# A third exponential tile and 15 KB more arena in a two-layer encoder kernel

## The chip, the cores and the metric

One NeuronCore of a Trainium2 chip runs the whole program. The metric is the device time of one execution in microseconds. Three executions of the kernel before took 1659.9, 1661.06 and 1663.4 us; the median, 1661.06 us, is the time before.

## What is computed

Two inputs A and B, each 1024 tokens by 1024 channels, pass through the same two layers. The reference, cut:

```
def even_layer(x, ...):
    h = rms_norm(x, norm_g)
    pu, pz, q, k, v, az = split(h @ w_in)           # 512, 512, 512, 128, 128, 512
    a_out = pool_mixer(pu, pool_w, pool_scale) * silu(pz)
    b_out = axial_gqa(q, k, v, q_g, k_g, tables) * silu(az)
    return x + concatenate([a_out, b_out]) @ w_out

def odd_layer(x, ...):
    h = rms_norm(x, norm_g)
    u, vv, z = split(h @ w_in, 3)
    vv = rms_norm(gelu(vv), sgu_g)
    sv = per chunk of 128 tokens, 8 groups: w_s @ vv + b_s
    return x + (gelu(u) * sv * silu(z)) @ w_out
```

The attention has 8 query heads of 64 channels on 2 key heads, full over the 1024 tokens, with normalised and rotated queries and keys. The pool mixer subtracts a token from the mean of a window (2, 4, 8 or 16 tokens) and mixes each group of 128 channels.

## The kernel before

**Numbers in two halves.** Each float32 operand of a matmul is scaled by a power of two and split into a float16 value and a float16 rest. A product takes three passes (`PASSES`, L383): high by high, high by rest, rest by high. The splitting is done by ScalarE (the rounding copy) and VectorE (the subtraction): L169 and L170 for weights, L365 and L366 for normalised inputs, L697 and L698 for probabilities, L753 to L756 for mixed values.

**Memory.** One large SBUF tile, the arena (`ARENA`, L33), holds nearly everything. `Arena.get` and `Arena.free` only note sizes and lifetimes; the kernel is traced, a planner (`make_plan`, `tried`, L76 to L116) gives each of the noted tiles an offset, and the kernel is traced again with them. The planner places large and long-lived tiles first, and each at the offset where the distance in time to the other users of that place is largest, counted up to 3.5% of the whole (`SLACK`); among equals it takes the lowest offset. The framework lays a wait wherever two tiles that share a place follow one another.

**Rings.** `consts_even` takes three rings out of the arena (L444 to L446), which live until the end of the second attention: transposed probabilities (3 tiles of 8 KB per partition), exponentials (`pf`, 2 tiles of 4 KB), and split probabilities (4 tiles of 4 KB). `Ring.get` hands the tiles out in turn.

**Attention.** `attention` (L660) runs four times for A and four times for B, each time for two heads, in rounds of 128 queries and one head: 16 rounds a call, 128 in all. A round is: four matmuls into a PSUM score tile of 128 by 1024 (L678; there are two such tiles), the maximum on VectorE (L684), the bias on ScalarE (L685), the exponential on ScalarE into a tile of the `pf` ring (L686), and a round later the split: a scaled row sum (L693), its reciprocal on VectorE (L695), the high half on ScalarE (L697), the rest on VectorE (L698), and a transposing transfer issued by SyncE (L699). For each 256 queries of the two heads 48 matmuls multiply values and probabilities (L710), and VectorE takes the result out (L714).

**Order.** Between the rounds `fill` (L335) runs chunks of other work out of a list by a nominal cost: projections, the pool mixer, norms of the other input, the output product of A, the beginning of its odd layer. Weights are fetched one block ahead (`Weights.fill`, L135): SyncE loads them (L153), VectorE takes the largest value (L252), and the two halves are made (L169, L170). All of the kernel's matmuls outside attention go through `mm` (L399). The order on each engine is not the order of the program text: the framework's scheduler lays it out ahead by its own estimate of times (`schedule_with_timeline_sim`, L1060), and each engine, and SyncE's queue of transfers, then keeps to it.

**After attention**, from about 920 us, come the rest of the odd layer's first product for A, the output product of B, and the odd layers of both.

SBUF also holds, at its low end, the space that the framework reserves for descriptors of transfers issued by GpSimd. The kernel before says nothing of it, and gets 16 KB per partition.

Of the kernel before, what the change touches and what calls it, by code (L numbers as in the profile page):

```python
# [10 lines left out]
F32 = mybir.dt.float32  # L11
# [9 lines left out]
P = 128  # L21
L = 1024
# [7 lines left out]
PAD = 8  # L30
W_PAD = L + 2 * PAD
RING = 96
ARENA = 186 * 1024  # L33
GRAIN = 512


class Arena:
# [3 lines left out]
    def __init__(self, nc, pool, plan=None):  # L41
        self.tile = pool.tile([P, ARENA // 4], F32, name="arena")
        self.nc, self.plan = nc, plan
        self.spans, self.held, self.now = [], {}, 0.0
# [45 lines left out]
def tried(spans, order, end):  # L90
    placed, plan = [], [None] * len(spans)
    for i in order:
# [3 lines left out]
        holes, last = [], 0  # L96
        for lo, hi in clash + [(ARENA, ARENA)]:
            if lo - last >= g:
# [101 lines left out]
class Kernel:  # L200
# [207 lines left out]
    def consts_even(self):  # L408
        nc = self.nc
        self.rope = {}  # L410
        cs = self.get([P, 2, NT, HD], F32)
        nc.sync.dma_start(out=cs, in_=self.rope_cs)
        ds = []
        for name, row in (("k", self.k_norm), ("q", self.q_norm)):
            g = self.tiny([P, 2, HD], keep="gain_" + name)
            nc.sync.dma_start(out=g[:, 0, :], in_=row.rearrange("(o n) -> o n", o=1).broadcast_to([P, HD]))
            gv = g[:, 0, :].rearrange("p (h s i) -> p h s i", h=2, s=2)
            gw = g[:, 1, :].rearrange("p (h s i) -> p h s i", h=2, s=2)
            for s in range(2):
                nc.vector.tensor_copy(out=gw[:, :, s, :], in_=gv[:, :, 1 - s, :])  # L420
            am = self.tiny([P, 1])
            self.amax(am, g[:, 0, :])
            d, s = self.scales(am, 1, 11, "g" + name, across=False)
            nc.vector.tensor_scalar(out=g, in0=g, scalar1=s[:, 0:1], scalar2=None, op0=ALU.mult)
            t = self.get([P, 2, NT, HD], F32, long=True)
            for i in range(2):
                nc.gpsimd.tensor_tensor(out=t[:, i], in0=cs[:, i], in1=g[:, i:i + 1, :].broadcast_to([P, NT, HD]), op=ALU.mult)
            self.rope[name] = t
            ds.append(d)
        self.free(cs)  # L430
        self.s_scale = self.tiny([P, 1], keep="s_scale")
        nc.vector.tensor_scalar(out=self.s_scale, in0=ds[0], scalar1=ds[1][:, 0:1], scalar2=HD ** -0.5, op0=ALU.mult, op1=ALU.mult)
        self.s_neg = self.tiny([P, 1], keep="s_neg")
        nc.vector.tensor_scalar(out=self.s_neg, in0=self.s_scale, scalar1=-1.0, scalar2=None, op0=ALU.mult)
        raw = self.get([P, 4, P], F32)
        nc.sync.dma_start(out=raw, in_=self.pool_w.rearrange("g c d -> c g d"))
        nc.vector.tensor_copy(out=self.pw[:, 0], in_=raw)
        nc.vector.tensor_tensor(out=self.pw[:, 1], in0=raw, in1=self.pw[:, 0], op=ALU.subtract)
        self.free(raw)
        self.pscale = self.tiny([P, 4], keep="pscale")  # L440
        nc.sync.dma_start(out=self.pscale, in_=self.pool_scale.rearrange("(g p) -> p g", p=P))
        self.edge = self.tiny([P, 4, 2, 8], keep="edge")
        nc.sync.dma_start(out=self.edge, in_=self.edges)
        self.pt = Ring(self, 3, [P, 2, NT, 256], F16)  # L444
        self.pf = Ring(self, 2, [P, L], F32)
        self.phl = Ring(self, 4, [P, 2, L], F16)  # L446

    def rotated(self, *args):
# [562 lines left out]
@with_exitstack  # L1011
def trunk_kernel(ctx: ExitStack, tc: tile.TileContext, args, order, plan):
    k = Kernel(ctx, tc, args, order, plan)
    k.run()
    k.arena.finish()
    return k.wts.order, k.arena.spans
# [32 lines left out]
def _trace(shapes, order=None, plan=None):  # L1049


    import concourse.bacc as _bacc

    nc = _bacc.Bacc("TRN2", target_bir_lowering=False, num_devices=1)
    args = {n: nc.dram_tensor("in_" + n, s, F32, kind="ExternalInput").ap() for n, s in shapes.items()}
    args["xs"] = [args.pop("x_prompt"), args.pop("x_sample")]
    args["outs"] = [nc.dram_tensor(f"out_{i}", (L, D), F32, kind="ExternalOutput").ap() for i in range(2)]
    noted = None
    try:
        with tile.TileContext(nc, schedule_with_timeline_sim=True) as tc:  # L1060
            noted = trunk_kernel(tc, args, order, plan)
            if plan is None:
                raise _Noted
    except _Noted:
        pass
    return nc, noted


def _planned(shapes):
    order, _ = _trace(shapes)[1]  # L1070
    return order, make_plan(_trace(shapes, order)[1][1])
# [15 lines left out]
```

## Time and profile before

| | before |
|---|---|
| median of three runs | 1661.06 us |
| the profiled execution, its span | 1660.36 us, 1658.3 us |
| PE busy | 1510.0 us, 91%, 11751 matmuls |
| PE weight load busy | 1025.5 us, 62% |
| DVE busy | 1064.1 us, 64% |
| ACT busy | 726.7 us, 44% |
| POOL busy | 121.1 us, 7% |
| data queue (SyncE) | 215.90 MB, 56.4% of 16 engines' span |
| mean granted TensorE clock | 0.963 |

PE is TensorE, DVE VectorE, ACT ScalarE, POOL GpSimd, SP SyncE. The profile is of one execution; its waits are worked out from semaphore events, and a wait for several things is put down to the one that came last. A mean over the span hides that the stages have different limits.

### The profile page before, as it was taken

The numbers are of one execution on the slowest core, as the hardware profiler recorded it, in microseconds if no ns is written. First come the engines' busy times: TensorE is split into PE (matmuls) and PEld (weight loads), VectorE is DVE, ScalarE is ACT, GpSimd is POOL, SyncE is SP. The second block draws the span as 40 slices with busy tenths as digits, with TensorE's granted clock in tenths as the row PEclk, the third lists the DMA queues.
The fourth block names the chain that finished last, engine by engine and source line by source line (L and its number), as shares of the span: only waits on it lengthen the run. The fifth ranks groups of instructions, "written<-read, shape, count | busy, mean of one in ns | idle before, by whom it ended". The sixth has DMA issues, their size and how long they took to land.

```text
span 1658.3 us, 28057 instructions
## 1 busy us (share of the span) xinstructions
PE 1510.0 (91%) x11751; PEld 1025.5 (62%) x11751; DVE 1064.1 (64%) x1613; ACT 726.7 (44%) x1121; POOL 121.1 (7%) x187
## 2 busy tenths in 40 slices
PE   2989899967779899999789899999979999998999
PEld 2745554646545777565468788554468655467888
DVE  7798999886897665798965754556660634344221
ACT  4366676766554555566655720224442513111000
POOL 2410010111100000010200200001100100000000
PEclk9999999978979999999899999999999999999999
DMA  9557787999866877787796453126511113224121
GB/s 237 122 120 151 148 149 148 197 202 181 182 134 146 191 182 170 158 162 145 191 213 155 127 186 99 42 77 140 127 52 39 39 38 102 70 90 140 64 84 52
DMA packets 497151, 217.69 MB, mean 131 GB/s; under 512 B 366336, under 2 KB 488704, under 8 KB 497024
## 3 DMA queue, kind: packets, MB, share of 16 engines
q1 hardware_dynamic: 497024, 215.90, 56.4%
q8 instruction: 92, 1.51, 0.4%
q14 instruction: 35, 0.29, 0.1%
HBM read 101.04 MB, written 24.12 MB: 75 GB/s over the span
## 4 chain that ended last, share of the span: by engine, by line
PE 37%; DVE 6%; DMA 5%; ACT 3%; issue 1%; POOL 0%; SPq 0%; DVEq 0%; ACTq 0%
PE bank L399 24%; PE ps_s L399 13%; DMA arena<-in_w_in_o 3%; DMA arena<-arena 1%; DVE arena L170 1%; ACT arena L169 1%; DVE arena L366 1%; DVE arena L364 1%; DMA arena<-in_w_out_e 1%; ACT arena L362 0%; DVE ring_weights L252 0%; DVE kept L252 0%; PE bank L710 0%; DVE arena L903 0%; DVE ring_attention L684 0%
## 5 line engine op out<-in xcount | busy, mean ns | idle before, releaser
L399 PEld LDWEIGHTS <-arena 128*128 128x128 f16 x9600 | 870.9, 99 | 458.7 <-DMA arena<-arena 34.6
L399 PE MATMUL bank<-arena 128*128 128x256 f16 (+2 forms) x8064 | 949.2, 279 | 47.7 <-DMA arena<-arena 14.0
L399 PE MATMUL ps_s<-arena 128*128 128x512 f16 x1536 | 335.5, 379 | 0.0
L169 ACT ACTIVATE arena<-arena,kept 128x1024 f16<-128x1024 f32 x108 | 122.2, 1144 | 327.1 <-DVE kept L281 125.7
L170 DVE SCALAR_TENSOR_TENSOR arena<-arena,kept 128x1024 f16<-128x1024 f32 x108 | 138.2, 1287 | 133.5 <-ACT arena L169 132.9
L698 DVE SCALAR_TENSOR_TENSOR arena<-arena,ring_attention 128x1024 f16<-128x1024 f32 x128 | 163.5, 1278 | 30.6 <-ACT arena L697 26.8
L686 ACT ACTIVATE arena<-ps_s,ring_attention,kept 128x1024 f32<-128x1024 f32 x128 | 153.8, 1201 | 38.9 <-DVE ring_attention L695 17.8
L678 PE MATMUL ps_s<-arena 128*128 128x512 f16 x512 | 138.7, 398 | 32.6 <-ACT arena L686 28.6
L684 DVE TENSOR_REDUCE ring_attention<-ps_s 128x1 f32<-128x1024 f32 x128 | 154.9, 1215 | 16.4 <-PE ps_s L678 15.8
L697 ACT ACTIVATE arena<-arena,ring_attention 128x1024 f16<-128x1024 f32 x128 | 145.8, 1141 | 36.8 <-DVE ring_attention L695 33.6
L784 DVE SCALAR_TENSOR_TENSOR arena<-bank,ring_dout,arena 128x512 f32<-128x512 f32 x64 | 47.6, 747 | 140.5 <-PE bank L399 139.6
L710 PE MATMUL bank<-arena 128*64 128x256 f16 x1536 | 110.1, 296 | 30.2 <-DMA arena<-arena 26.4
L710 PEld LDWEIGHTS <-arena 128*64 128x64 f16 x1536 | 93.5, 120 | 55.3 <-DMA arena<-arena 26.5
L252 DVE TENSOR_REDUCE ring_weights<-arena 128x1 f32<-128x1024 f32 x58 | 70.6, 1216 | 80.3 <-DMA arena<-in_w_in_o 36.4
L678 PEld LDWEIGHTS <-arena 128*128 128x128 f16 x512 | 48.1, 100 | 94.1 <-issue 47.2
L685 ACT ACTIVATE ring_attention<-ring_attention,kept 128x1 f32<-128x1 f32 x128 | 36.9, 290 | 132.8 <-DVE ring_attention L684 132.5
L364 DVE SCALAR_TENSOR_TENSOR arena<-arena,ring_norm 128x1024 f32<-128x1024 f32 x32 | 41.0, 1280 | 19.5 <-POOL ring_norm L318 19.3
L838 ACT ACTIVATE arena<-bank,ring_dvv 128x256 f32<-128x256 f32 x64 | 26.7, 467 | 56.3 <-PE bank L399 52.2
L362 ACT ACTIVATE arena<-arena 128x1024 f32<-128x1024 f32 x32 | 33.6, 1052 | 36.0 <-DMA arena<-in_x_prompt 13.9
L884 DVE SCALAR_TENSOR_TENSOR arena<-bank,kept,arena 128x512 f32<-128x512 f32 x32 | 22.9, 748 | 39.6 <-PE bank L399 39.6
L365 ACT CAST arena<-arena 128x1024 f16<-128x1024 f32 x32 | 33.3, 1040 | 33.9 <-DVE arena L364 33.7
L315 POOL TENSOR_SCALAR ring_norm<-ring_norm 128x1 f32<-128x1 f32 x32 | 12.7, 398 | 467.7 <-ACT arena L362 458.1
(104 smaller groups left out, 888.3 us busy)
## 6 DMA issues: line engine op xcount, KB each, us to landing
arena<-in_w_in_o SPq DMA_DIRECT2D x48, 512.0 KB, 4.1
arena<-in_w_in_e SPq DMA_DIRECT2D x36, 512.0 KB, 4.7
arena<-in_w_out_e SPq DMA_DIRECT2D x16, 512.0 KB, 5.2
x<-arena SPq DMA_DIRECT2D x32, 256.0 KB, 3.2
arena<-x SPq DMA_DIRECT2D x16, 512.0 KB, 4.3
arena<-x SPq DMA_DIRECT2D x32, 256.0 KB, 2.9
out<-arena SPq DMA_DIRECT2D x32, 256.0 KB, 2.1
mixed<-arena SPq DMA_DIRECT2D x14, 512.0 KB, 3.7
```

The costliest lines, as they stand in the source:

```text
L169: nc.scalar.activation(out=hi, in_=raw, func=AF.Copy, scale=s[:, 0:1])
L170: nc.vector.scalar_tensor_tensor(out=lo, in0=raw, scalar=s[:, 0:1], in1=hi, op0=ALU.mult, op1=ALU.subtract)
L252: self.nc.vector.tensor_reduce(out=out, in_=in_, axis=axis, op=ALU.max, apply_absolute_value=True)
L364: nc.vector.scalar_tensor_tensor(out=x, in0=x, scalar=r[:, 0:1], in1=gain[0], op0=ALU.mult, op1=ALU.mult)
L399: self.nc.tensor.matmul(out=o, lhsT=l, rhs=r, start=first and i == 0, stop=last and i == n - 1)
L678: nc.tensor.matmul(out=ps[:, half * 512:half * 512 + 512], lhsT=st.qT[j][:, tt, h, :], rhs=st.kT[:, 4 * half:4 * half + 4, kv, a, :], star ...
L684: nc.vector.tensor_reduce(out=m, in_=ps, axis=AX.X, op=ALU.max)
L686: nc.scalar.activation(out=p, in_=ps, func=AF.Exp, scale=self.s_scale[:, 0:1], bias=nb[:, 0:1], accum_out=ss)
L697: nc.scalar.activation(out=hl[:, 0, :], in_=p, func=AF.Copy, scale=r[:, 0:1])
L698: nc.vector.scalar_tensor_tensor(out=hl[:, 1, :], in0=p, scalar=r[:, 0:1], in1=hl[:, 0, :], op0=ALU.mult, op1=ALU.subtract)
L710: nc.tensor.matmul(out=ps[h * HD:h * HD + HD, :], lhsT=st.v[:, a, t, kv * HD:kv * HD + HD], rhs=pts[g, h][:, b, t, :], start=n < 2, stop=n ...
L784: nc.vector.scalar_tensor_tensor(out=res, in0=ps.rearrange("p (t n) -> p t n", t=2), scalar=box["d"][:, 0:1], in1=res, op0=ALU.mult, op1=A ...
```

## The change

The space for descriptors is set to 1 KB. The arena takes the 15 KB, and the ring of exponentials gets a third tile of 4 KB out of the arena. The planner runs anew with both. No instruction of the kernel's text is added, removed or moved.

```diff
-ARENA = 186 * 1024
+ARENA = 201 * 1024
...
         self.pt = Ring(self, 3, [P, 2, NT, 256], F16)
-        self.pf = Ring(self, 2, [P, L], F32)
+        self.pf = Ring(self, 3, [P, L], F32)
         self.phl = Ring(self, 4, [P, 2, L], F16)
...
-    nc = _bacc.Bacc("TRN2", target_bir_lowering=False, num_devices=1)
+    nc = _bacc.Bacc("TRN2", target_bir_lowering=False, num_devices=1, dynamic_dma_scratch_size=1024)
```

## Rows read from the trace of the kernel before

**Rows 1.** Busy time by stage: us, then busy us per engine, clock, DMA share, GB/s
```profile
core 0: us, PE busy (x) PEld busy (x) DVE busy (x) ACT busy (x) POOL busy (x), PEclk, DMA share, GB/s
...
100.00:300.00 200.00, 184.39 (x1271) 100.21 (x1270) 183.05 (x309) 136.87 (x236) 7.15 (x10) 0.96 0.74 148
300.00:420.00 120.00, 96.08 (x934) 71.64 (x934) 94.64 (x129) 79.60 (x132) 21.82 (x34) 0.85 1.00 199
...
440.00:480.00 40.00, 21.75 (x186) 14.32 (x187) 30.69 (x52) 23.75 (x42) 1.94 (x3) 0.74 0.92 202
480.00:790.00 310.00, 298.14 (x2489) 200.57 (x2487) 235.88 (x332) 171.61 (x282) 13.96 (x20) 0.99 0.76 160
790.00:850.00 60.00, 44.77 (x280) 29.73 (x279) 51.03 (x68) 41.90 (x73) 12.30 (x21) 0.86 0.85 198
...
920.00:1658.00 738.00, 713.05 (x5153) 489.98 (x5151) 334.46 (x463) 187.33 (x223) 29.32 (x48) 0.99 0.29 85
sum 1658.00, PE 1509.99 PEld 1025.54 DVE 1064.12 ACT 726.67 POOL 121.09; mean PE 167.78 PEld 113.95 DVE 118.24 ACT 80.74 POOL 13.45
```

**Rows 2.** Who TensorE waited for, whole span: us in total, times, longest us
```profile
PE ps_s L678 <- ACT arena L686: 28.6, 15, 3.9
PE bank L710 <- DMA arena<-arena: 26.4, 15, 5.5
PE bank L399 <- DMA arena<-arena: 14.0, 7, 2.7
PE bank L399 <- ACT arena L169: 13.1, 3, 7.7
...
PE bank L399 <- DMA arena<-in_w_in_o: 4.2, 1, 4.2
```

**Rows 3.** The same view, 0 to 40 us
```profile
PE bank L399 <- ACT arena L169: 10.1, 2, 7.7
```

**Rows 4.** DMA queues of the page: kind, packets, MB, share
```profile
q1 hardware_dynamic: 497024, 215.90, 56.4%
```

**Rows 5.** Timeline of one round: start us, us, instruction, idle before and releaser
```profile
457.13 1.28 DVE L698 SCALAR_TENSOR_TENSOR arena<-arena,ring_attention 128x1024 f16<-128x1024 f32 x1
457.25 0.29 ACT L685 ACTIVATE ring_attention<-ring_attention,kept 128x1 f32<-128x1 f32 x1 [1.89 <-DVE ring_attention L684]
...
458.53 1.21 ACT L686 ACTIVATE arena<-ps_s,ring_attention,kept 128x1024 f32<-128x1024 f32 x1 [0.98 <-DVE ring_attention L695]
...
459.87 1.01 PE L678 MATMUL ps_s<-arena 128*128 128x512 f16 x2 [3.92 <-ACT arena L686]
```

**Rows 6.** What the exponential's line waited for: us, times
```profile
  DVE ring_attention L695: 17.8, 15
  DVE arena L698: 8.9, 11
```

**Rows 7.** Timeline, three exponentials and the scores that waited for them
```profile
114.62 1.20 ACT L686 ACTIVATE arena<-ps_s,ring_attention,kept 128x1024 f32<-128x1024 f32 x1 [0.80 <-DVE ring_weights L265]
...
115.96 1.02 PE L678 MATMUL ps_s<-arena 128*128 128x512 f16 x4 [1.97 <-ACT arena L686]
...
346.83 1.20 ACT L686 ACTIVATE arena<-ps_s,ring_attention,kept 128x1024 f32<-128x1024 f32 x1 [0.98 <-DVE arena L698]
...
348.18 1.87 PE L678 MATMUL ps_s<-arena 128*128 128x512 f16 x4 [3.47 <-ACT arena L686]
...
474.18 1.21 ACT L686 ACTIVATE arena<-ps_s,ring_attention,kept 128x1024 f32<-128x1024 f32 x1 [0.98 <-DVE ring_attention L695]
...
475.53 1.86 PE L678 MATMUL ps_s<-arena 128*128 128x512 f16 x4 [2.37 <-ACT arena L686]
```

**Rows 8.** Busy time by stage, after the exponential at 346.83
```profile
347.00:360.00 13.00, 7.36 (x43) 4.00 (x43) 12.74 (x17) 10.13 (x16) 0.00 (x0) 0.50 1.00 185
```

**Rows 9.** Who ScalarE waited for, 440 to 480 us
```profile
ACT arena L686 <- DVE ring_attention L695: 7.6, 6, 1.7
```

**Rows 10.** Groups by line: count, busy us, mean ns, idle before
```profile
L684 DVE TENSOR_REDUCE ring_attention<-ps_s 128x1 f32<-128x1024 f32 x128 | 154.9, 1215 | 16.4 <-PE ps_s L678 15.8
```

## The prediction

> **What bounds the kernel now.** I read the stages first, then who TensorE waits for, then single rounds of the timeline.
>
> The busy time by stage [rows 1] splits the span in two. From 920 us on TensorE is busy 713.05 of 738 us at a mean clock of 0.99: that half is bound by its matmuls, and more room changes nothing there that I can price. Before it lies the attention of both inputs. There TensorE stands still for 15.6 us between 100 and 300, 23.9 between 300 and 420, 18.3 between 440 and 480, 11.9 between 480 and 790 and 15.2 between 790 and 850: 84.9 us in all, each the window less PE busy. The reason differs. From 100 to 300 VectorE is busy 183.05 of 200 us and TensorE 184.39, both 92%: nearly full. From 300 to 420 the DMA share is 1.00: transfers bind. From 440 to 480 TensorE is at 54%, VectorE at 77%, ScalarE at 59%; DMA, at 0.92, is close to full, and the rest is latency, with the clock at a mean of 0.74, so that for about half of this stretch it stood at 1.2 GHz.
>
> Who TensorE waits for [rows 2]: 28.6 us in 15 waits for the exponential at L686, which must free a PSUM score tile before new scores can be written; 26.4 us in 15 waits of the probability-times-values matmuls (L710) for transposed probabilities; 14.0 us for other transposes; 13.1 us for converted weights (L169), of which 10.1 fall into the first 40 us [rows 3], and 4.2 us for a weight transfer.
>
> **The change part by part.**
>
> *Descriptor space, 16 KB to 1 KB.* The data moves in one hardware queue, 497024 packets and 215.90 MB [rows 4], and the kernel issues every transfer from SyncE (`nc.sync`), none from GpSimd. Nothing uses the space that is cut. Cost 0, from both sides: no instruction is added or taken away.
>
> *Three exponential tiles for two.* An exponential writes tile p; the two halves of the split (L697 on ScalarE, L698 on VectorE) read it. With two tiles the exponential i waits until L698 of i-2 has read its tile. One round of the timeline shows the wait [rows 5]: the bias of the exponential is ready at 457.54 (457.25 + 0.29), but the L698 that started at 457.13 ends at 458.41, and the exponential starts at 458.53 after 0.98 us of idling. The profile names a reciprocal (L695) as the releaser, because that came last on VectorE; the exponential reads nothing of it, and what holds its tile is the L698 that ended 0.12 us before the start. TensorE then gets its score tile at 459.87, after 3.92 us. With a third tile this exponential needs L698 of i-3, long done.
>
> All such waits on ScalarE: 17.8 us put down to L695 and 8.9 to L698, 26.7 us before 26 of the 128 exponentials [rows 6]. ScalarE is no bound, so what counts is what TensorE gets of it. Seven of the 15 waits of TensorE for an exponential have an exponential that had itself been late behind VectorE; of each I take the smaller of the two idle times: 0.80, 0.98, 0.33, 0.28, 0.98, 0.98, 0.98, together 5.33 us. The first and the last of the seven and the one at 346.83 are shown [rows 7], and the sixth is the round above. The one at 346.83 comes off: VectorE is busy 12.74 of the 13 us that follow [rows 8], so scores that come earlier wait for it. Leaves 4.35. In the stretch from 440 to 480 six exponentials wait 7.6 us [rows 9]; 1.96 of that is counted, and the other 5.6 delay the split, the transpose and thereby L710. I take half, 2.8, because the DMA share of 0.92 can absorb the other half. Ring: 4.35 + 2.8 = 7.2 us. The ends: 0 if the next thing in order (L684 on VectorE, the transposes) is late by as much, and 28.6 us if every wait for an exponential goes.
>
> Nothing is added to any queue by the ring: the instructions are the same, and no new wait arises. [...]
>
> *Arena 186 KB to 201 KB.* The ring takes 4 of the 15 KB, 11 remain during attention, 15 after it. The planner places every tile anew. What it can save directly is the wait for weights after the start, 13.1 - 10.1 + 4.2 = 7.2 us [rows 2, 3]. I take 1 us: the 4.2 is a transfer issued late in a stretch with a DMA share of 0.85, and weights are fetched one block ahead by the program's order, which more space does not change. From 300 to 420 a norm of the second input could start a load or two earlier (a tile is 4 KB), but that only moves bytes within stretches of 1.00 and 0.74. Ends: 7.2 us gained; a loss can come only through a new order of work, and is priced with the second rival, since the planner has more places to choose from for each tile, not fewer.
>
> Sum, against the profiled execution's own 1660.36 us (span 1658.3 and 2.06 around it): 1660.36 - 7.2 - 1.0 = 1652.2. The median of the runs is 1661.06, 0.7 above it: 1652.9, so 1653 us.
>
> **The rivals.**
>
> *No measurable change (1661 us).* The waits that go are on ScalarE, and in 100 to 300 two other engines are at 92%, in 300 to 420 DMA is at 1.00; only the 40 us at 440 are latency-bound, and there DMA is at 0.92. If transfers hold that stretch, the 2.8 us of my sum and the 1.96 of the waits there are lost, and what remains is 4.35 - 1.96 + 1.0 = 3.4 us, which is just at the limit of what can be told from no change; where VectorE takes back those 2.4 us as well, nothing remains. For it: the occupancy. Against it: L698 ends at 458.41 and the exponential starts at 458.53, a plain wait. [...]
>
> *Slower, later transposes (1666 to 1675, say 1670 us).* The order on each engine is not the program's but one laid out ahead by the framework from its own estimates, and it changes when a dependency goes. With two tiles the exponential i can't be planned before L698 of i-2. With three, the row maximum of the next scores (L684, 1215 ns [rows 10]) can be put ahead of an L698 that today precedes it. The transpose of that row block then starts 1.22 us later, and so does L710, whose 15 waits for transposes already cost 26.4 us. If it hits all 15: 18.2 us, less the 4.35 gained, 1675; if half, 9.1 - 4.35 = 4.8, 1666. It decides from four of the 15 on (4 x 1.22 = 4.9 against 4.35), and shows as slower from seven. For it: TensorE is slowed by its gaps as well, since the clock is 0.74 to 0.86 in the stretches that have most of them. Against it: an earlier exponential makes its own split ready earlier, and VectorE has slack at 440 to 480. A re-laid arena has the same effect on the order of SyncE's queue, where transfers stand in line behind transposes; this is in the same case.
>
> *Much faster (1640 us).* The stretch from 440 to 480 fills: its 18.3 us of idle TensorE go, and with the 2.4 us of the other waits (4.35 - 1.96) that makes 20.7. Against it: the DMA share of 0.92 there leaves 3.2 of 40 us for what would have to move up.
>
> *The change doesn't do what it says.* The planner may leave the distances between two users of a place as they are, and the order may still hold exponentials behind L698; then it is the no-change case.
>
> **How the numbers follow.** Forecast (1653) 0.42, much faster (1640) 0.10, no change 0.20, slower (1670) 0.28. Two runs of this kernel can be told apart from about 0.2%, 3.3 us: faster 0.52, same 0.20, slower 0.28. The forecast's own range is 1646 to 1658 (the ring with the arena's 7.2 us, or 3 us of it all). The range for 8 in 10 runs from 1638 to 1672: it takes in the gain of 20.7 us and most of the slower case, leaving about 0.05 below and 0.10 above.
>
> **What would show it.** Right: idle time before L686 put down to L695 and L698 falls from 26.7 us to a few, TensorE's waits for L686 fall from 28.6 by 4 to 7, TensorE's busy share between 440 and 480 rises, and the part from 920 on keeps its length of 738 us within 2. Wrong: the waits of L710 for transposes grow beyond 26.4 us and the attention ends later than 920 (second rival); the ring's wait is gone but L684 or L710 have taken it over at the same total (no change); or the time after 920 moves, which would mean that the arena and not the ring decides. The forecast fails as a whole if the order of L684 and L698 on VectorE turns out to be changed throughout.

## The result, and the profile after

The changed kernel takes 1622.45 us (median of four runs, 1619.84 to 1624.01) against 1661.53 us: ratio 0.9763, 95% interval 0.9748 to 0.9779. That is 39 us faster. The direction was forecast, the size not: 1653 was the forecast and 1638 the lower end of the range. The profiled execution took 1619.84 us, the fastest of the four, with a span of 1618.1.

The same stages as in [rows 1], for the kernel after: window, its length, busy time of PE, PEld, DVE, ACT and POOL with counts, granted clock, DMA share, GB/s.

```profile
...
100.00:300.00 200.00, 184.55 (x1287) 99.68 (x1286) 189.31 (x321) 143.11 (x242) 10.10 (x18) 0.97 0.79 157
300.00:420.00 120.00, 104.86 (x1058) 74.76 (x1057) 108.67 (x165) 83.97 (x143) 20.48 (x30) 0.96 1.01 205
420.00:440.00 20.00, 12.89 (x103) 7.63 (x103) 12.79 (x17) 14.45 (x28) 1.83 (x2) 0.83 1.03 238
440.00:480.00 40.00, 33.21 (x262) 20.42 (x262) 37.75 (x59) 26.51 (x43) 3.41 (x3) 0.83 0.54 99
480.00:790.00 310.00, 292.57 (x2374) 195.34 (x2373) 235.42 (x332) 169.06 (x277) 14.32 (x26) 0.98 0.75 170
790.00:850.00 60.00, 51.16 (x442) 40.87 (x441) 47.11 (x66) 40.68 (x72) 6.35 (x12) 0.94 1.04 240
...
920.00:1618.00 698.00, 684.50 (x4925) 465.34 (x4923) 307.77 (x432) 160.29 (x188) 23.59 (x43) 0.99 0.28 81
sum 1618.00, PE 1496.48 PEld 1014.14 DVE 1061.80 ACT 728.99 POOL 117.31; mean PE 166.28 PEld 112.68 DVE 117.98 ACT 81.00 POOL 13.03
```

TensorE stands still for 15.5, 15.1, 6.8, 17.4 and 8.8 us in the five attention windows of [rows 1], 63.6 in all where it was 84.9. Between 420 and 440, which is not among them, it stands still for 7.1 us where it was 1.3, so part of what 440 to 480 won has only moved. The clock went from 0.85 to 0.96 between 300 and 420 and from 0.74 to 0.83 between 440 and 480. Over the span the mean clock rose from 0.963 to 0.976; with the two levels of 1.2 and 2.4 GHz that is an estimated 2 x (1 - 0.963) x 1658.3 = 122.7 us at the lower one before, and 77.7 after. The same 11751 matmuls keep TensorE busy for 1496.48 us where it was 1509.99: 13.5 of the 40.2 us of span are shorter busy time, which goes with the higher clock, and 26.7 are idle time that went. Fixed windows hold different work in the two kernels, so a second division is needed: the last result of attention (L714, the 32nd) falls at 911.0 us before and at 885.2 after, and what follows takes 747.3 us before and 732.9 after. Of the 40.2 us of span, 25.8 are won up to the end of attention and 14.4 behind it.

Who TensorE waited for, in the kernel after (us in total, times, longest), against [rows 2]:

```profile
PE bank L710 <- DMA arena<-arena: 34.3, 15, 7.6
PE ps_s L678 <- ACT arena L686: 21.5, 14, 3.0
PE bank L290 <- DVE diag L270: 16.2, 3, 10.5
PE bank L399 <- ACT arena L169: 12.7, 2, 7.7
PE bank L399 <- DMA arena<-arena: 5.6, 5, 2.2
```

In the kernel before, the longest line of that view is one that [rows 2] leaves out. It is the matmul that spreads a largest value over all partitions, which the scales are made from:

```profile
PE bank L290 <- DVE diag L270: 28.9, 7, 10.6
```

Of this, 16.2 us lie in the first 100 us, in both kernels; 8.4 us lie behind attention in the kernel before, and nothing in the kernel after.

And the exponential's line, against [rows 6]:

```profile
  DVE ring_attention L695: 3.7, 4
  DVE arena L698: 1.4, 2
```

The exponential's waits on these two lines fell from 26.7 to 5.1 us, and TensorE's waits for exponentials fell by 7.1 us, from 28.6. Its waits for transposes at L710 grew from 26.4 to 34.3 us. So neither of these two lines carries the 39 us; the two cancel.

One of the gains behind attention, 8.42 of the 14.4 us, can be read line by line. It is the end of A's odd layer, where the scale of the mixed values needs the last column block. First the kernel before, ScalarE's and then TensorE's timeline (start us, length us, instruction, idle before and releaser), and the same time in the chain that ended last (start us, us, what):

```profile
1211.64 1.15 ACT L169 ACTIVATE arena<-arena,kept 128x1024 f16<-128x1024 f32 x1 [7.00 <-DMA arena<-in_w_in_o]
1214.14 1.15 ACT L169 ACTIVATE arena<-arena,kept 128x1024 f16<-128x1024 f32 x1 [1.35 <-DVE arena L170]
1215.19 1.10 ACT L902 ACTIVATE arena<-ps_s,ring_duz 128x1024 f32<-128x1024 f32 x1
```

```profile
1207.01 5.40 PE L399 MATMUL bank<-arena 128*128 128x256 f16 x48
1220.83 0.27 PE L290 MATMUL bank<-diag,ones 128*128 128x128 bf16 x1 [8.42 <-DVE diag L270]
```

```profile
1204.96 1.15 DVE arena L903
...
1206.12 5.44 DMA arena<-in_w_in_o
...
1211.64 1.16 ACT arena L169
```

TensorE finished the last product of this block (L399 into `ps_s`) at 1207, but its activation L902 stands in ScalarE's queue behind two weight conversions, L169, of which the first waits 7.00 us for its weights; the chain shows why they are late: their transfer begins at 1206.12, right behind an L903 on VectorE that ends there, and takes 5.44 us. By the chain this L903 is what released the transfer: it has nothing to do with these weights but to use the place that they were given. The planner's list agrees: the two tiles for this block of weights lie on places of the tile that L903 reads last (`z` in `z_chunks`), given up 1.8% and 1.1% of the planner's time before; in the change the last users of the two places are 4.0% and 4.4% away. L902 comes at 1215.19, and TensorE stands still for 8.42 us before the scale's matmul L290. In the kernel after:

```profile
1177.24 1.11 ACT L902 ACTIVATE arena<-ps_s,ring_duz 128x1024 f32<-128x1024 f32 x1 [5.73 <-PE ps_s L399]
```

```profile
1182.28 3.19 PE L399 MATMUL ps_s<-arena 128*128 128x512 f16 x14
1185.31 0.22 PE L290 MATMUL bank<-diag,ones 128*128 128x128 bf16 x1
```

L902 starts when its own input is there, no conversion stands before it, and L290 has no wait. A place that was given up too late turned into a stall of TensorE by way of two queues, neither of which shows a wait of TensorE on weights.

### The profile page after: what moved, and what is told of

Read it like the earlier page. It is cut to its first block, busy times and chain, and to the rows that moved or that the text cites. A ratio compares the mean times of both kernels' runs of the same rounds, so it can differ in the third digit from the quotient of the medians.

```text
span 1618.1 us, 28061 instructions
## 1 busy us (share of the span) xinstructions
PE 1496.5 (92%) x11751; PEld 1014.1 (63%) x11751; DVE 1061.8 (66%) x1613; ACT 729.0 (45%) x1121; POOL 117.3 (7%) x187
## 4 chain that ended last, share of the span: by engine, by line
PE 57%; DVE 16%; DMA 11%; issue 4%; ACT 4%; POOL 1%; SPq 1%; DVEq 0%; ACTq 0%; POOLq 0%
PE bank L399 35%; PE ps_s L399 17%; DMA arena<-arena 4%; PE bank L710 3%; DVE arena L698 3%; DVE ring_attention L684 3%; PE ps_s L678 3%; DMA arena<-in_w_in_e 2%; DMA arena<-in_w_in_o 1%; DMA arena<-x 1%; ACT arena L686 1%; DVE ring_weights L252 1%; DVE arena L170 1%; DVE arena L756 1%; DVE arena L622 1%
## 5 line engine op out<-in xcount | busy, mean ns | idle before, releaser
L399 PEld LDWEIGHTS <-arena 128*128 128x128 f16 x9600 | 863.9, 99 | 434.1 <-DMA arena<-arena 25.6
L399 PE MATMUL bank<-arena 128*128 128x256 f16 (+2 forms) x8064 | 941.1, 277 | 31.8 <-ACT arena L169 12.7
L399 PE MATMUL ps_s<-arena 128*128 128x512 f16 x1536 | 338.1, 380 | 2.4 <-DVE arena L170 2.4
L169 ACT ACTIVATE arena<-arena,kept 128x1024 f16<-128x1024 f32 x108 | 121.4, 1142 | 281.1 <-DVE kept L281 126.2
L698 DVE SCALAR_TENSOR_TENSOR arena<-arena,ring_attention 128x1024 f16<-128x1024 f32 x128 | 163.2, 1278 | 31.3 <-ACT arena L697 29.9
L684 DVE TENSOR_REDUCE ring_attention<-ps_s 128x1 f32<-128x1024 f32 x128 | 155.0, 1216 | 10.8 <-PE ps_s L678 10.5
L678 PE MATMUL ps_s<-arena 128*128 128x512 f16 x512 | 136.8, 394 | 26.2 <-ACT arena L686 21.5
L686 ACT ACTIVATE arena<-ps_s,ring_attention,kept 128x1024 f32<-128x1024 f32 x128 | 153.7, 1201 | 8.4 <-DVE ring_attention L695 3.7
L710 PE MATMUL bank<-arena 128*64 128x256 f16 x1536 | 107.7, 290 | 35.7 <-DMA arena<-arena 34.3
L710 PEld LDWEIGHTS <-arena 128*64 128x64 f16 x1536 | 90.2, 117 | 61.2 <-DMA arena<-arena 31.6
L678 PEld LDWEIGHTS <-arena 128*128 128x128 f16 x512 | 47.9, 100 | 81.1 <-issue 38.6
L364 DVE SCALAR_TENSOR_TENSOR arena<-arena,ring_norm 128x1024 f32<-128x1024 f32 x32 | 41.8, 1306 | 25.7 <-POOL ring_norm L318 22.7
L362 ACT ACTIVATE arena<-arena 128x1024 f32<-128x1024 f32 x32 | 33.7, 1054 | 53.1 <-DMA arena<-x 32.9
L903 DVE TENSOR_TENSOR arena<-arena 128x1024 f32<-128x1024 f32 x16 | 19.6, 1223 | 51.2 <-ACT arena L902 51.2
L838 ACT ACTIVATE arena<-bank,ring_dvv 128x256 f32<-128x256 f32 x64 | 26.7, 466 | 54.8 <-PE bank L399 53.9
L902 ACT ACTIVATE arena<-ps_s,ring_duz 128x1024 f32<-128x1024 f32 x16 | 17.7, 1109 | 66.8 <-PE ps_s L399 66.8
```

The lines of the kernel that those rows point to most:

```text
L169: nc.scalar.activation(out=hi, in_=raw, func=AF.Copy, scale=s[:, 0:1])
L364: nc.vector.scalar_tensor_tensor(out=x, in0=x, scalar=r[:, 0:1], in1=gain[0], op0=ALU.mult, op1=ALU.mult)
L399: self.nc.tensor.matmul(out=o, lhsT=l, rhs=r, start=first and i == 0, stop=last and i == n - 1)
L678: nc.tensor.matmul(out=ps[:, half * 512:half * 512 + 512], lhsT=st.qT[j][:, tt, h, :], rhs=st.kT[:, 4 * half:4 * half + 4, kv, a, :], star ...
L684: nc.vector.tensor_reduce(out=m, in_=ps, axis=AX.X, op=ALU.max)
L686: nc.scalar.activation(out=p, in_=ps, func=AF.Exp, scale=self.s_scale[:, 0:1], bias=nb[:, 0:1], accum_out=ss)
```

## The experiments

The edits are to the kernel before, unless "the change" is named. Sizes are KB per partition; the space for descriptors is cut so that arena and descriptors together stay at 202 (187 in scratch_only, 202.5 in arena202).

**One part at a time.**

```diff
# ring_only: every tile keeps its place of before, the third tile lies behind them (arena 190)
+        self.tile = pool.tile([P, (ARENA + 4096) // 4], F32, name="arena")
...
+        if self.arena.plan:
+            self.arena.plan.insert(len(self.arena.spans), ARENA)
+            self.pf.tiles.append(self.get([P, L], F32, long=True))
# arena_only
-ARENA = 186 * 1024
+ARENA = 201 * 1024
# scratch_only
+    ... num_devices=1, dynamic_dma_scratch_size=1024)
# ring_in_186
-        self.pf = Ring(self, 2, [P, L], F32)
+        self.pf = Ring(self, 3, [P, L], F32)
```

Expected of ring_only:

> Before's arena places are kept one by one; only a third exponential tile lies behind them, at 186 KB. Theory (room): most of the 39 us come from the larger arena, so this gives 1648 to 1658 us, the 7 us of my sum or less. Rival (ring): the third tile makes the gain, 1622 to 1635. Second rival (order): whatever changes a dependency draws a new order, and this lands anywhere between 1622 and 1665.

Expected of arena_only:

> Arena of 201 KB, ring of two exponential tiles. Theory (room): 1622 to 1635 us. Rival (ring): 1652 to 1661. Second rival (order): anywhere between 1622 and 1665.

Expected of scratch_only:

> Descriptor space of 1 KB, arena of 186 KB and ring of two: the same instructions in the same order, 15 KB lower in SBUF. All theories: 1661 us within 0.2%, idle before L686 near 26.7 us as before.

Expected of ring_in_186:

> Three exponential tiles inside the old 186 KB, the planner runs anew with 4 KB less for the rest. Theory (room): 1655 to 1670 us, since room is taken away. Rival (ring): 1625 to 1640. Second rival (order): anywhere between 1622 and 1670.

| | median us | ratio | 95% | end of attention | the rest |
|---|---|---|---|---|---|
| before | 1661.06 | | | 911.0 | 747.3 |
| the change | 1622.45 | 0.9763 | 0.9748 to 0.9779 | 885.2 | 732.9 |
| ring_only | 1662.01 | 1.0009 | 1.0 to 1.0019 | 912.2 | 749.6 |
| arena_only | 1633.2 | 0.9837 | 0.9821 to 0.9853 | 903.3 | 725.2 |
| scratch_only | 1660.53 | 1.0003 | 0.999 to 1.0015 | | |
| ring_in_186 | 1661.59 | 1.0015 | 1.0002 to 1.0028 | 929.3 | 730.1 |

The descriptor space costs and gains nothing. The third tile alone gains nothing, with the other places kept or planned anew; for the former 1648 to 1658 had been expected. The arena alone gains 27 us (0.0163 of 1661.24). It does so although the ring's wait is still there, and larger than before; the line of the exponential in arena_only:

```profile
  DVE ring_attention L695: 22.6, 18
  DVE arena L698: 19.8, 17
...
  PE ps_s L678: 39.7, 15
```

In ring_only it is the reverse. The ring's waits are gone, but TensorE waits longer for the exponentials, 55.1 us where it was 28.6 (this kernel's lines stand three lower: L689 is L686 and L681 is L678):

```profile
  DVE ring_weights L265: 1.8, 1
  DVE ring_attention L698: 0.9, 1
  DVE arena L701: 0.8, 2
...
  PE ps_s L681: 55.1, 21
```

The first rival of the pair, the ring as the main cause, has fallen. The 11 us between arena_only and the change come only with the third tile; how much of them is the tile's own is taken up below.

**How much room.** Both sizes of ring, with arenas in between:

```diff
-ARENA = 186 * 1024
+ARENA = 190 * 1024   # ring3_190; 195 in ring3_195; with the ring of three
+ARENA = 192 * 1024   # ring2_192; 197 in ring2_197; with the ring of two
```

Expected of ring3_190:

> Three tiles, arena 190 KB planned anew: the other tiles have just the room of before. Theory (room): attention ends between that of three tiles in 186 KB (929 us) and that of the change (885), near 911 as before, total 1635 to 1655. Rival (order): total anywhere in 1620 to 1665 and no order among the sizes.

Expected of ring3_195:

> Three tiles, arena 195 KB: half of the added room. Theory (room): below the time with 190 KB and above that with 201, 1625 to 1645, attention ends near 898. Rival (order): no relation to the size.

Expected of ring2_192:

> Two tiles, arena 192 KB. Theory (room): between 1661 and 1633, attention ends at 903 to 911. Rival (order): anywhere from 1620 to 1665.

Expected of ring2_197:

> Two tiles, arena 197 KB: the other tiles have the same room as in the change, so that only the third tile is missing. Theory (room, and the third tile pays only with room): 1630 to 1640, attention ends near 903, that is some 10 us more than the change. Rival (order): anywhere from 1620 to 1665.

"Room" is the arena less 4 KB for each tile of the ring. The last two columns are counted from the planner's own list of lifetimes and offsets: how many of the some 555 tiles that lie on a place used earlier get it within 1% and within 2% of the planner's whole time after its last user gave it up. That time is counted in matmul columns; 1% is 16.6 us on average.

| | room | median us | ratio, 95% | within 1% | within 2% |
|---|---|---|---|---|---|
| ring_in_186 | 174 | 1661.59 | 1.0015 | 132 | 286 |
| before | 178 | 1661.06 | | 113 | 287 |
| ring3_190 | 178 | 1657.35 | 0.9982, 0.9968 to 0.9996 | 113 | 279 |
| ring3_195 | 183 | 1646.95 | 0.9917, 0.988 to 0.9954 | 98 | 240 |
| ring2_192 | 184 | 1654.65 | 0.9948, 0.993 to 0.9966 | 90 | 239 |
| ring2_197 | 189 | 1630.17 | 0.981, 0.9782 to 0.9839 | 87 | 208 |
| the change | 189 | 1622.45 | 0.9763 | 87 | 203 |
| arena_only | 193 | 1633.2 | 0.9837 | 79 | 188 |

The time falls as the room grows, with either ring, though not from each step to the next: at 193 KB and two tiles it is longer than at 189 KB and three. Ring3_190 came out above its 1635 to 1655 and ring3_195 just above its 1625 to 1645. At equal room of 189 KB the third tile is worth 7.7 us, at 178 KB 3; ring_in_186, where it takes the others' room, gains nothing.

**What of the room acts.** If it is the distance in time between two users of a place, the gain must vanish when the arena stays large but the planner no longer looks for distance. `SLACK` is the distance beyond which it is content.

```diff
-SLACK = 0.035
+SLACK = 0.005   # near_half, on the change; 0.010 in near_one, 0.020 in near_two
```

Expected of near_half:

> The change with SLACK 0.005: 201 KB and three tiles stay, but the planner is content with a distance of 0.5% of its time between two users of a place, and takes low offsets. Theory (distance: room pays because a tile's place was given up longer ago): 1660 us or more, the whole gain gone. Rival (room as such, by more tiles alive or by the new order): 1620 to 1635.

Expected of near_one:

> The same with SLACK 0.010: places given up at least 1% of the planner's time ago (about 17 us) where possible. Theory (distance): between 1622 and the time at 0.005; nearer to 1622 if only users closer than 17 us cost time. Rival: 1620 to 1635.

Expected of near_two:

> The same with SLACK 0.020, about 33 us. Theory (distance): 1620 to 1635, since almost no wait of a transfer or an engine reaches back so far. Rival: also 1620 to 1635; it is the series of the three that tells.

| on the change | median us | ratio, 95% | within 1% | within 2% |
|---|---|---|---|---|
| near_half | 1665.75 | 1.0027, 1.0011 to 1.0043 | 232 | 457 |
| near_one | 1648.97 | 0.9924, 0.9889 to 0.9958 | 83 | 424 |
| near_two | 1634.07 | 0.9841, 0.979 to 0.9892 | 88 | 195 |
| SLACK 0.035 | 1622.45 | 0.9763, 0.9748 to 0.9779 | 87 | 203 |

With all the space on offer and the third tile, and places reused early, everything is lost. So space does not pay by itself; it pays by the distances that the planner makes of it. The two are not quite parted, since a planner that is soon content also leaves the added space empty: by its list 23 tiles reach above 186 KB in near_half, 44 in near_one, 83 in near_two and 90 in the change. No count alone orders the times either: near_one has as few tiles within 1% as the change. The step from near_one to near_two, 15 us, suggests that a place given up 17 us ago is still too fresh, but it is little more than the 12 us that other places at nearly equal distances make (below). That near_two is 12 us behind the change with nearly the same counts is not explained by distance.

```diff
# room_attention, on the change: tiles taken after the end of the second attention stay below 186 KB
+        top = min(ARENA, 186 * 1024) if t0 > RINGS_END else ARENA
+        clash = [(lo, hi) for lo, hi in clash if lo < top]
...
-        for lo, hi in clash + [(ARENA, ARENA)]:
+        for lo, hi in clash + [(top, ARENA)]:
...
+        RINGS_END = self.arena.now
```

Expected of room_attention:

> The change, but tiles taken after the end of the second attention stay within the first 186 KB. If the added room pays within attention alone: 1622 to 1630, attention ends near 885 us and the rest takes 733. If the part after attention needs it too: attention as in the change, the rest 740 to 750 us as before, in all 1630 to 1640.

It took 1632.79 us (0.9833, 0.9777 to 0.9889): attention ends at 885.7 as in the change, the rest takes 742.3. So the two halves gain separately. But ring_in_186 needs only 730.1 for the rest with 186 KB, where before takes 747.3 with the same: behind attention, other places in the old room can win as much as the added room does.

**Waits that fall away, or another order?** A new set of places changes the waits, and from them the scheduler lays out another order. Where the old order breaks no new wait, it can be kept by edges that fix the order of issue and wait for nothing.

```diff
# ring_same_order: before's places, third tile at 186 KB, all engines and SyncE in before's order
...
+                for lane in lanes:
+                    for a, b in zip(lane, lane[1:]):
+                        tc.add_manual_dep(traced[b], a, info, reason="order")
# pe_order: the change, the same edges for TensorE's instructions alone
```

Expected of ring_same_order:

> Before's places, a third exponential tile at 186 KB, and every engine and SyncE's queue held to before's order: what the third tile does by its waits alone. The step of my sum: 1661 - 7.2 = 1654 us, with idle time before L686 near 0. Rival (nothing waits on the exponentials for long enough): 1660 to 1662. If it is 1654, the re-drawn order took the gain away from the third tile in the run that had only that.

Expected of pe_order:

> The change, but TensorE held to the order of before (the other engines are ordered anew around it). If the gain comes from waits on places that fall away: 1622 to 1640. If it comes from the order in which TensorE takes its work: 1655 to 1665.

Ring_same_order takes 1658.49 us, 0.9983 (0.9973 to 0.9994) of before, between the 1654 of the sum and the 1660 to 1662 of the rival: the third tile's waits alone are worth 2.8 us (1.0 to 4.5). ScalarE never idles before the exponential, and TensorE's waits for it go from 28.6 to 25.9 us, while those for transposes rise from 26.4 to 32.9:

```profile
PE bank L710 <- DMA arena<-arena: 32.9, 17, 5.5
...
PE ps_s L678 <- ACT arena L686: 25.9, 14, 4.2
```

Pe_order takes 1657.41 us, 0.9977 (0.9962 to 0.9991), as expected if TensorE's order makes the gain. Up to the last L714 and behind it (columns as above), first the kernel before, then the change, then pe_order:

```profile
0.00:911.00 911.00, 787.94 (x6517) 527.50 (x6518) 725.60 (x1144) 538.50 (x896) 91.77 (x139) 0.94 0.79 168
911.00:1658.00 747.00, 722.05 (x5235) 498.04 (x5235) 338.52 (x469) 188.17 (x225) 29.32 (x48) 0.99 0.30 87
```

```profile
0.00:885.20 885.20, 777.18 (x6509) 517.60 (x6510) 727.62 (x1149) 541.18 (x896) 88.93 (x139) 0.96 0.80 174
885.20:1618.00 732.80, 719.30 (x5244) 496.54 (x5242) 334.18 (x465) 187.81 (x225) 28.38 (x48) 0.99 0.30 87
```

```profile
0.00:923.70 923.70, 782.36 (x6518) 521.05 (x6519) 729.01 (x1149) 541.55 (x896) 95.23 (x139) 0.94 0.77 166
923.70:1656.80 733.10, 717.02 (x5235) 495.41 (x5233) 334.18 (x465) 187.57 (x225) 29.82 (x48) 1.00 0.30 87
```

With the places of the change, but its own work in the old order, TensorE ends attention at 923.7 us, 12.7 later than before: without TensorE's new order none of the 25.8 us is there. That waits which fall away are worth nothing is not shown by this, since the other engines follow an order in this run that is neither the old one nor that of the change, and it may cost something of its own. Behind attention it is the other way round: with TensorE in the old order, the rest takes 733.1 us, as in the change. There, in the rows at 1207 us, it was ScalarE's and SyncE's queues that stalled. No run keeps the order of all engines with the new places, so waits and order are not parted further.

**How far does the draw go?**

```diff
-SLACK = 0.035
+SLACK = 0.040   # change_far40 on the change, before_far40 on before
```

Expected of change_far40:

> The change with SLACK 0.040: nearly the same distances between users of a place (198 of 554 within 2% of the planner's time, 203 in the change), but other places and another order. Theory (distance): 1620 to 1636. Rival (a lucky order in the change): back to 1640 or more.

Expected of before_far40:

> The kernel before with SLACK 0.040: the same 186 KB and two tiles, other places (269 of 557 within 2%, 287 in before) and another order. Theory (distance): 1648 to 1665. Rival (an unlucky order in before): 1625 to 1645.

Change_far40 took 1634.39 us (0.984, 0.9807 to 0.9873), before_far40 1665.45 (1.0022, 1.0009 to 1.0034), half a us above its range. Other places at nearly equal distances move the time by 12 and by 4 us. The small arena stays slow and the large one fast.

**More room still.**

```diff
# split3, on the change
-        self.phl = Ring(self, 4, [P, 2, L], F16)
+        self.phl = Ring(self, 3, [P, 2, L], F16)
# arena202, on the change
-ARENA = 201 * 1024
+ARENA = 202 * 1024   # descriptors 512 bytes
```

Expected of split3:

> The change with three split-probability tiles and not four: the other tiles get 4 KB more, and 188 of 553 tiles follow within 2% on the last user of their place (203 in the change). Theory (distance): 1615 to 1634. If the fourth split tile is needed, since a transpose must have read a tile before it is written again: 1640 to 1660.

Expected of arena202:

> The change with an arena of 202 KB and 512 bytes for descriptors: distances as in the change. Theory (distance, with a draw of the order that moves the time by some 12 us): 1622 to 1636. Rival (the change's order is at the end of what room gives): 1622.

1624.25 us (0.9779, 0.9736 to 0.9822) and 1624.46 (0.978, 0.9721 to 0.9839): as fast as the change, not faster. The fourth split tile is not needed here. Arena202 is hardly a draw of its own: 573 of its 593 tiles lie where they lie in the change. Split3 and change_far40 are, and with the change they give 1624, 1634 and 1622 us: the change is no single lucky draw, though it is the best of three.

Split3 also makes a pair with arena_only. Its 592 tiles have the same sizes, lifetimes and places, one by one; only that one 4 KB tile of the ring of split probabilities serves as a third exponential. It takes 1624.25 us, arena_only 1633.2: 9 us, from the tile and the order that goes with it.

Where the gain falls differs from draw to draw. In the seven runs with 197 KB or more and SLACK 0.020 to 0.040 that leave places and orders free (the change, arena_only, ring2_197, near_two, change_far40, split3 and arena202), by their profiled executions, attention ends 3.5 to 25.8 us earlier than before, and the rest is 14.4 to 22.1 us shorter. The change has the most in attention and the least behind it.

## Why the prediction was wrong

**The stages** were read rightly: attention has the idle TensorE, and in the change most of the gain is there, though in arena_only it is 7.7 of 29.8 us. "More room changes nothing there that I can price" for the part from 920 us on was wrong by 14.4 us. I took a mean of 97% busy for a bound by matmuls and left out the 8.42 us of stall. It is one of the seven waits in the longest line of the view of [rows 2], L290 for L270, which I did not list.

**Descriptor space, 0 us:** right, 1660.53 us.

**The third tile, 7.2 us:** the mechanism was right, the wait goes. The size was too large: 2.8 us (1.0 to 4.5) with the order kept, where transposes take back what the exponentials give. Neither part of the 7.2 came in full: TensorE's waits for exponentials fell by 2.7 us where I counted 4.35, and those for transposes rose by 6.5 where I counted on 2.8 less. With the order free and the old room it gains 0 (ring_only) to 3 us (ring3_190); with the new room 7.7 us (ring2_197 to the change) and 9 (arena_only to split3).

**The arena, 1.0 us:** this is the step that failed. It measured 27 us alone, and 31.6 with 197 KB (0.019 of 1661.63). The step asked which waits of TensorE name a weight, found 7.2 us, and took a part. It treated the order of each engine as given. Within attention none of the gain is there without TensorE's new order, as pe_order tells, and behind it the wait sat on ScalarE in front of something else. Neither can be read off TensorE's waits for weights. My sentence that weights are fetched one block ahead "by the program's order, which more space does not change" was wrong in its premise, since the scheduler issues what its places allow. The sum also has no term for the clock: 13.5 of the 40.2 us are busy time of TensorE that the same matmuls no longer need.

**The second rival** priced a new order as a loss only. That a new order comes was right, and in ring_only it took the ring's gain as that rival said, though by waits for exponentials and not by later transposes (25.7 us, before 26.4). Its own mechanism, L684 put ahead of L698, is no more frequent than before: over the 128 rounds, VectorE has taken 0, 1, 2 or 3 later maxima ahead of a round's L698 27, 47, 45 and 9 times before, and 28, 50, 40 and 10 times in the change. That the same freedom could gain 30 us had no case at all; the range ended at 1638 because the fastest case filled one stretch of 40 us.

**The mark "the time after 920 moves, which would mean that the arena and not the ring decides"** could not tell. Counted from a fixed time, the part behind it (738 us before, 698 after) is the span less 920 and falls with any gain. Counted from the last L714 it fell from 747.3 to 732.9 us, so something behind attention did move; but in ring_in_186, with a third tile in the old arena, it fell to 730.1.

The Trainium skill, page Perfetto Trace Analysis, section Identifying Performance Opportunities, says that the same gap repeating on the engine that should be saturated can mean too little SBUF. Here the gap that repeated was on ScalarE, which is not that engine, and filling it was worth 2.8 us. SBUF was indeed short, but in the arena, and TensorE's waits show no gap of one size: those for exponentials in [rows 5, 7] are 1.97, 3.47, 2.37 and 3.92 us, and the stall behind attention came once.

What stays open is which places in attention bind the order. Sums of waits do not tell: ScalarE's waits for weight transfers before L169 fell from 118.2 us to 58.9 in the change, but near_half has 75.6 and is as slow as any. The share of the third tile at full room (7.7 us between ring2_197 and the change, 9 between arena_only and split3) lies within what a draw moves (12 us).

## What to carry to other kernels

Where a planner places tiles and a scheduler lays out the order, judge a change of space by how soon places are reused, counted from the planner's list, and not by the waits of one engine that the trace happens to show: those are what is left after the order was laid around the reuse. The counts tell a tight plan from a loose one; they did not tell times within 12 us apart. The sum of the waits on an engine off the path promises more than their removal gives (26.7 us of waits, 2.8 us of time); a run with the order held fixed measures it. And before a stage is called bound by its busy share, look for its few long gaps one by one.

## What the runs showed that was not expected

Holding only TensorE to the old order costs 35 of the 39 us that the change gained (1657.41 against 1622.45 us) with all other engines free to follow. And the time of a kernel of this kind moves by 4 to 12 us with places that are nearly equally far apart, as much as its runs spread and up to three times that (1619.84 to 1624.01 us), so that a single pair of variants a few us apart says nothing about the edit between them.
